# A two-layer hybrid decoder on one core: the adaLN vectors of the gates and of the shared K/V move from TensorE strips to VectorE sums, and one pair of gates moves to the last head

## The chip, the core and the metric

The kernel runs on one core of a Trainium2 chip. The metric is the device time of one launch in microseconds (us). Before the change the median of three runs is 934.68 us (934.39 to 935.48). Engines are named as in the profile: PE is TensorE, PEld its weight loads, DVE VectorE, ACT ScalarE, POOL GpSimd, SP the queue that issues the large loads.

## The reference, cut to what matters

Two decoder layers on 256 tokens of width 1024. Layer 0 mixes with an mLSTM block of four heads, layer 1 with causal attention over shared K and V; each then has a mixture of 16 experts. Everything is conditioned on one vector c: a product with a 1024 x 14336 matrix gives 14 vectors of 1024, the shift, scale and gate of every sub-layer and the shift and scale of K/V.

```python
cond = jax.nn.silu(c) @ w_ada + b_ada            # 14 vectors of 1024
mods = cond[:, :n_layer_mod].reshape(B, DEPTH, 2, 3, D)   # 0-11
kv_mod = cond[:, n_layer_mod:].reshape(B, 2, D)           # 12, 13
for layer in range(DEPTH):
    shift, scale, gate = mods[:, layer, 0, 0], mods[:, layer, 0, 1], 1.0 + mods[:, layer, 0, 2]
    h = x * (1 + scale) + shift
    y = mlstm_layer(h, ...) if layer == 0 else moba_layer(h, ..., shared K/V)
    x = layer_norm(DEEPNORM_ALPHA * x + gate * y, ...)
    shift, scale, gate = mods[:, layer, 1, 0], mods[:, layer, 1, 1], 1.0 + mods[:, layer, 1, 2]
    y = moe_ffn(x * (1 + scale) + shift, ...)
    x = layer_norm(DEEPNORM_ALPHA * x + gate * y, ...)
```

So vector 3i is a shift, 3i+1 a scale and 3i+2 a gate: 2 and 5 are the gates of layer 0, 8 and 11 those of layer 1, and 12, 13 are shift and scale of K/V.

## The kernel before, in words

The tokens lie in two tiles of 128. The program has four stretches: the start and the mLSTM of layer 0 (to about 316 us), its experts (to about 535 us), the attention of layer 1 (to about 691 us) and its experts. In the two mixers every weight tile (512 KB, loaded on SP's queue into a ring of 20 slots) is split in two halves: ScalarE copies the high part (L265), VectorE subtracts it for the low part (L266), and TensorE makes three matmuls of each product (L274, L275, L276).

Between these products the 14 conditioning vectors are worked off, each from 8 tiles of 128 x 1024 of w_ada. Vectors 0 and 1 come first. For the others there are two ways:

- `ada_vector` (L353): VectorE multiplies a tile by a column of silu(c) (L360) and adds seven more to it (L362); three steps later TensorE sums over the partitions with a block of ones, in four strips of 32 output partitions (L368); `ada_columns` (L340) copies that to an SBUF tile `mr` on ScalarE (L343), two steps later turns it by transposes (L348), and VectorE adds the bias (L350).
- `ada_pair` (L372): TensorE multiplies the tiles of two vectors as they come, four strips of 32 output partitions for each of 8 steps (L379, tile `adapp`), with nothing on VectorE. A pair of gates stays in rows in a tile `hl` (L387, L388); the pair (12, 13) goes through `ada_columns`.

A gate is spread to all partitions by `gate_rows` (L433): two matmuls for each half of 512 (L439), and one pass on ScalarE (L440).

The order of this work is set by `pump` (L402), which is called before every step of the large products: it gives a running vector a credit of RATE for each call, starts a pair when the count of calls reaches the pair's number, and moves what waits for its transposes one step on. `queue` (L426) sets what is to be done: 3, 4, 6, 7 by vectors and the pairs (2, 5) at call 8 and (12, 13) at call 46 in layer 0; 9, 10 by vectors and the pair (8, 11) at call 20 in layer 1. What is left over is worked off at once by `ada_all` (L418), which is called in `before_moe` (L456) and just behind it, ahead of the last products of a mixer (L935, L936 and L1519, L1520).

```python
RATE = (0.25, 0.33, 0.33)
PAIRS = ((2, 5, 8), (12, 13, 46)), ((8, 11, 20),)
```

Of the kernel before, what the change touches and what calls it, by code (L numbers as in the profile page):

```python
# [9 lines left out]
F32 = mybir.dt.float32  # L10
# [25 lines left out]
EXTRA = 4  # L36
RATE = (0.25, 0.33, 0.33)
PAIRS = ((2, 5, 8), (12, 13, 46)), ((8, 11, 20),)
WA = 3
# [118 lines left out]
def _body(ctx, tc, x, w_ada, a_w_in, a_wq, a_wk, a_wv, a_w_out, b_w_kv, b_wq, b_wo, moe_w_gate, moe_w_up,  # L158
# [161 lines left out]
    A.activation(csil, csil, AF.Silu)  # L320
    gaterow = {}
    before = keep.tile([P, P], BF16, name="before")
# [17 lines left out]
    def ada_columns(j, n, ps):  # L340

        mr = small.tile([P, P * n], F32, tag=("cv" if n == 2 else "lntmp"), name=f"mr{j}")
        A.copy(mr, ps)  # L343
        yield 0
        yield 0
        pt = bankB(f"adat{j}")
        for b in range(n):
            T.transpose(pt[:, P * b:P * b + P], mr[:, P * b:P * b + P], ident)  # L348
        o = slice(KD * j, KD * j + 4 * n)
        V.tensor_tensor(mod.rearrange("p j k -> p (j k)")[:, o].rearrange("p (g b) -> p g b", g=4),  # L350
                        pt[:, 0:P * n].rearrange("p (b g z) -> p g b z", b=n, g=4)[:, :, :, 0],
                        K("bada")[:, o].rearrange("p (g b) -> p g b", g=4), op=OP.add)

    def ada_vector(j, delay=3):
# [14 lines left out]
        busy.clear()  # L369
        yield from ada_columns(j, 2, ps[:, 0:256])  # L370

    def ada_pair(j, i):  # L372
# [12 lines left out]
        else:  # L385
            hl = keep.tile([P, 512], F32R, tag="shared", name=f"mr{j}")
            A.copy(hl, ps)  # L387
            V.scalar_tensor_tensor(hl, hl.bitcast(F32), C("low"), ps, op0=OP.mult, op1=OP.add)  # L388
            gaterow[j], gaterow[i] = (hl, 0), (hl, 2)

# [42 lines left out]
    def gate_rows(j):  # L433
        gt = keep.tile([P, D], F32, tag="gate", name=f"gate{j}")
        hl, g = gaterow[j]
        for h in range(2):
            pg = bankB(f"adag{j}_{h}")
            for r, v in ((16 + 2 * (j // 3) + h, lnr), (24 + g + h, hl)):
                T.matmul(pg, pick[:, r:r + 1].to_broadcast([P, P]), v, start=(v is lnr), stop=(v is hl))  # L439
            A.activation(gt[:, 512 * h:512 * h + 512], pg, AF.Identity, bias=ones)  # L440
# [370 lines left out]
    for _ in start_dense(3, range(1, 3)):  # L811
        pass
    queue((3, 4, 6, 7), RATE[0], PAIRS[0])
    for h in range(1, NH):
# [650 lines left out]
    with tc.issue_after(end.ins):  # L1465
        queue((9, 10), RATE[2], PAIRS[1])
        k_part(0)
# [100 lines left out]
```

## Time and profile before

| | |
|---|---|
| median of 3 runs | 934.68 us (934.39 to 935.48) |
| profiled execution: its time, its span | 936.49 us, 934.8 us |
| TensorE busy, mean granted clock | 884.2 us (95%), 0.980 |
| VectorE, ScalarE busy | 497.2 us (53%), 330.1 us (35%) |
| DMA | 318.57 MB, 341 GB/s over the span |

Matmuls are pipelined and the profile models their ends, so a share of 95% on TensorE says that something is in the array, not that it works at its peak. The shares are means over four stretches with different limits; so the stretches are read one by one, and within them the idle time of an engine together with what ended it.

### The profile page before, as it was taken

The numbers are of one execution on the slowest core, as the hardware profiler recorded it, in microseconds if no ns is written. First come the engines' busy times: TensorE is split into PE (matmuls) and PEld (weight loads), VectorE is DVE, ScalarE is ACT, GpSimd is POOL, SyncE is SP. The second block draws the span as 40 slices with busy tenths as digits, with TensorE's granted clock in tenths as the row PEclk, the third lists the DMA queues.
The fourth block names the chain that finished last, engine by engine and source line by source line (L and its number), as shares of the span: only waits on it lengthen the run. The fifth ranks groups of instructions, "written<-read, shape, count | busy, mean of one in ns | idle before, by whom it ended". The sixth has DMA issues, their size and how long they took to land. (4 is left out here: it accounts for less than half of the span.)

```text
span 934.8 us, 13546 instructions
## 1 busy us (share of the span) xinstructions
PE 884.2 (95%) x5141; PEld 537.4 (57%) x5144; DVE 497.2 (53%) x929; ACT 330.1 (35%) x547; POOL 7.8 (1%) x21
## 2 busy tenths in 40 slices
PE   9998999998999799999999889999979999999975
PEld 4885798695877544434343369577755443434322
DVE  2475877477788743233333289478675323333317
ACT  3465565364657311111111046376642111111110
POOL 0020000000000000000000000000000000000000
PEclk9999999998999999999999999999998999999988
DMA  9999976499757969999999999985685999999991
GB/s 329 390 392 406 351 266 218 135 393 392 254 196 272 359 237 407 407 405 407 407 407 406 377 410 416 412 301 207 250 313 210 407 406 407 406 407 407 407 393 59
DMA packets 161921, 318.57 MB, mean 341 GB/s; under 512 B 10120, under 2 KB 28168, under 8 KB 161848
## 3 DMA queue, kind: packets, MB, share of 16 engines
q1 hardware_dynamic: 161704, 317.42, 90.3%
q8 instruction: 43, 0.70, 0.3%
q14 instruction: 30, 0.25, 0.1%
q10 hardware_dynamic: 144, 0.20, 0.1%
HBM read 316.53 MB, written 1.05 MB: 340 GB/s over the span
## 5 line engine op out<-in xcount | busy, mean ns | idle before, releaser
L135 PE MATMUL py<-w,aT 128*64 128x512 f32 (+1 forms) x576 | 118.4, 554 | 1.7 <-DMA w<-in_moe_w_down_dram 1.7
L135 PE MATMUL pu<-w,xe 128*64 128x512 f32 x512 | 118.5, 596 | 0.1
L135 PE MATMUL pg<-w,xe 128*64 128x512 f32 x512 | 116.1, 596 | 0.0
L1221 DVE SCALAR_TENSOR_TENSOR yl<-py,wsl,yh 128x512 fp32r<-128x512 f32 x28 | 21.0, 750 | 177.7 <-ACT yh L1220 177.7
L135 PEld LDWEIGHTS py<-w,aT 128*64 128x64 f32 x576 | 41.3, 139 | 74.6 <-issue 62.5
L135 PEld LDWEIGHTS pu<-w,xe 128*64 128x64 f32 x512 | 36.0, 137 | 67.1 <-issue 61.3
L135 PEld LDWEIGHTS pg<-w,xe 128*64 128x64 f32 x512 | 34.8, 137 | 64.0 <-issue 58.9
L1187 ACT COPY aT<-aT 128x512 f32<-128x512 f32 x16 | 9.4, 586 | 143.6 <-PE aT L135 143.6
L530 DVE TENSOR_TENSOR lntmpe<-po,gate 128x512 f32<-128x512 f32 x56 | 36.1, 685 | 39.9 <-PE po L135 39.9
L362 DVE SCALAR_TENSOR_TENSOR adacc<-ada,pk,adacc 128x1024 f32<-128x1024 f32 x42 | 53.7, 1278 | 0.2
L1220 ACT ACTIVATE yh<-py,wsl 128x512 fp32r<-128x512 f32 x28 | 19.2, 687 | 85.1 <-PE py L135 85.1
L508 ACT ACTIVATE xe<-ga,coef 128x256 f32<-128x256 f32 x32 | 16.1, 561 | 73.2 <-PE ga L135 63.2
L274 PE MATMUL z<-hh,wz 128*128 128x256 f32 x128 | 37.0, 289 | 0.0
L275 PE MATMUL z<-hl,wz 128*128 128x256 f32 x128 | 36.1, 282 | 0.0
L531 DVE TENSOR_TENSOR xt<-xt,lntmpe 128x512 f32<-128x512 f32 x56 | 36.0, 683 | 0.0
L276 PE MATMUL z<-hh,wz 128*128 128x256 f32 x128 | 36.0, 281 | 0.0
L135 PE MATMUL ga<-onehot,xh 128*128 128x256 f32 x128 | 31.8, 327 | 0.0
L379 PE MATMUL adapp<-ada,pk 128*32 128x512 f32 x192 | 30.5, 599 | 0.0
L1180 DVE TENSOR_TENSOR a<-a,pu 128x512 f32<-128x512 f32 x16 | 11.0, 689 | 36.0 <-PE pu L135 35.6
L135 PE MATMUL xm<-hh,win 128*128 128x256 f32 x144 | 28.8, 289 | 0.7 <-ACT hh L135 0.7
L135 PEld LDWEIGHTS ga<-onehot,xh 128*128 128x128 f32 x128 | 25.3, 223 | 5.6 <-DVE xt L531 4.1
L274 PE MATMUL y<-wo,av 128*128 128x512 f32 x60 | 24.7, 415 | 3.4 <-ACT av L270 3.4
(386 smaller groups left out, 1899.9 us busy)
## 6 DMA issues: line engine op xcount, KB each, us to landing
w<-in_moe_w_gate_dram SPq DMA_DIRECT2D x128, 512.0 KB, 10.2
w<-in_moe_w_up_dram SPq DMA_DIRECT2D x128, 512.0 KB, 10.2
w<-in_moe_w_down_dram SPq DMA_DIRECT2D x128, 512.0 KB, 10.2
ada<-in_w_ada_dram SPq DMA_DIRECT2D x112, 512.0 KB, 9.7
win<-in_a_w_in_dram SPq DMA_DIRECT2D x16, 512.0 KB, 8.4
wz<-in_a_w_in_dram SPq DMA_DIRECT2D x16, 512.0 KB, 6.6
wout<-in_a_w_out_dram SPq DMA_DIRECT2D x16, 512.0 KB, 7.1
wv<-in_a_wv_dram SPq DMA_DIRECT2D x8, 512.0 KB, 5.7
```

Of the source, the lines that this page charges most:

```text
L135: return self.tc.keep_in_program_order(f(*a, **kw))
L274: T.matmul(ps, l[0], r[0], start=start, stop=False, skip_group_check=True)
L275: T.matmul(ps, l[0], r[1], start=False, stop=False, skip_group_check=True)
L276: T.matmul(ps, l[1], r[0], start=False, stop=stop, skip_group_check=True)
L362: V.scalar_tensor_tensor(acc, w, c, acc, op0=OP.mult, op1=OP.add)
L379: T.matmul(ps[32 * g:32 * g + 32, :], csil[:, k:k + 1].to_broadcast([P, 32]), w[g // 2][:, 512 * (g % 2):512 * (g % 2) + 512], start=(k == ...
L508: A.activation(dst, ps, AF.Identity, bias=sh[:, k:k + 1], scale=sc[:, k:k + 1])
L530: V.tensor_tensor(tmp, y, gate[:, c], op=OP.mult)
L531: V.tensor_tensor(dst[:, t, c], dst[:, t, c], tmp, op=OP.add)
L1180: V.tensor_tensor(a, a, pu, op=OP.mult)
L1220: A.activation(yh, py, AF.Copy, scale=wsl[:, b:b + 1])
L1221: V.scalar_tensor_tensor(yl, py, wsl[:, b:b + 1], yh.bitcast(F32), op0=OP.mult, op1=OP.subtract)
```

## The change

In layer 0 vectors 12 and 13 are now made as 3, 4, 6 and 7 are, by VectorE; the pair (2, 5) stays on TensorE but starts at call 44. In layer 1 no pair is left: 8, 9, 10 and 11 are all made by VectorE, the gates 8 and 11 side by side in one tile `hl`. RATE goes up. `mr` has its own buffer (in work[0], where it was one of `small`'s shared ones), and the transposes come six steps after the copy, not two. The number of tiles and bytes loaded in each layer stays.

```diff
-RATE = (0.25, 0.33, 0.33)
-PAIRS = ((2, 5, 8), (12, 13, 46)), ((8, 11, 20),)
+RATE = (0.45, 0.35, 0.55)
+PAIRS = ((2, 5, 44),), ()
...
-        mr = small.tile([P, P * n], F32, tag=("cv" if n == 2 else "lntmp"), name=f"mr{j}")
+        mr = work[0].tile([P, P * n], F32, tag="mr", name=f"mr{j}")
         A.copy(mr, ps)
-        yield 0
-        yield 0
+        for _ in range(6):
+            yield 0
...
-        yield from ada_columns(j, 2, ps[:, 0:256])
+        if is_gate(j):
+            if j % 2 == 0:
+                gates.append(keep.tile([P, 512], F32R, tag="shared", name=f"mr{j}"))
+            gate_parts(j, gates[-1][:, 256 * (j % 2):256 * (j % 2) + 256], ps[:, 0:256], range(4))
+        else:
+            yield from ada_columns(j, 2, ps[:, 0:256])
+
+    def is_gate(j):
+        return j < 12 and j % 3 == 2
+
+    def gate_parts(j, hl, ps, groups):
+
+        A.copy(hl, ps)
+        V.scalar_tensor_tensor(hl, hl.bitcast(F32), C("low"), ps, op0=OP.mult, op1=OP.add)
+        gaterow[j] = hl, groups
...
-            hl = keep.tile([P, 512], F32R, tag="shared", name=f"mr{j}")
-            A.copy(hl, ps)
-            V.scalar_tensor_tensor(hl, hl.bitcast(F32), C("low"), ps, op0=OP.mult, op1=OP.add)
-            gaterow[j], gaterow[i] = (hl, 0), (hl, 2)
+            gate_parts(j, keep.tile([P, 512], F32R, tag="shared", name=f"mr{j}"), ps, (0, 1))
+            gaterow[i] = gaterow[j][0], (2, 3)
...
     def gate_rows(j):
...
-            for r, v in ((16 + 2 * (j // 3) + h, lnr), (24 + g + h, hl)):
-                T.matmul(pg, pick[:, r:r + 1].to_broadcast([P, P]), v, start=(v is lnr), stop=(v is hl))
+            r = 16 + 2 * (j // 3) + h
+            T.matmul(pg, pick[:, r:r + 1].to_broadcast([P, P]), lnr, start=True, stop=False, skip_group_check=True)
+            for i in range(n):
+                r = 24 + groups[n * h + i]
+                T.matmul(pg[:, 512 // n * i:512 // n * i + 512 // n], pick[:, r:r + 1].to_broadcast([P, P]), hl, start=False, stop=(i == n - 1),
+                         skip_group_check=True)
...
-    queue((3, 4, 6, 7), RATE[0], PAIRS[0])
+    queue((3, 4, 12, 13, 6, 7), RATE[0], PAIRS[0])
...
-        queue((9, 10), RATE[2], PAIRS[1])
+        queue((8, 9, 10, 11), RATE[2], PAIRS[1])
```

The order of instructions shows where the pieces now stand. The first place is TensorE's queue in the q product of head 0. Before:

```order
L274 MATMUL q_1_866<-ch_731,wq_0_867 128x256
L379 MATMUL adapp_943<-ada_0_00_944,pk 32x512 x2
L379 MATMUL adapp_943<-ada_0_00_946,pk 32x512 x2
L275 MATMUL q_0_865<-cl_732,wq_0_867 128x256
L276 MATMUL q_0_865<-ch_731,wq_0_867 128x256
```

Changed:

```order
L274 MATMUL q_1_866<-ch_731,wq_0_870 128x256
L275 MATMUL q_0_865<-cl_732,wq_0_870 128x256
L276 MATMUL q_0_865<-ch_731,wq_0_870 128x256
L274 MATMUL q_0_865<-ch_731,wq_0_870 128x256
L275 MATMUL q_0_865<-cl_732,wq_0_870 128x256
```

The four strips of the pair (2, 5) are gone from here and from nine other places in the q and k products of heads 0 and 1; all of them now stand together before the last head's k product, where those of (12, 13) stood.

The second place is VectorE's queue in layer 1, behind the splits of the first q product (`adacc` is a vector's sum, `qs` and `sb` belong to the attention's scores). Before:

```order
L266 TENSOR_TENSOR bq_4_5473<-wq_1_00_5407,bq_4_5473 128x1024
L266 TENSOR_TENSOR bq_6_5533<-wq_1_01_5409,bq_6_5533 128x1024
L1418 TENSOR_SCALAR qs_5085<-bq_0_5411 128x512
L1418 TENSOR_SCALAR qs_5086<-bq_1_5412 128x512
L1430 SCALAR_TENSOR_TENSOR sb_5578<-group_384_5088,s_5579 128x384
```

Changed:

```order
L266 TENSOR_TENSOR bq_4_5487<-wq_1_00_5412,bq_4_5487 128x1024
L266 TENSOR_TENSOR bq_6_5517<-wq_1_01_5414,bq_6_5517 128x1024
L360 TENSOR_SCALAR adacc_5468<-ada_0_00_5469,pk 128x1024
L383 SCALAR_TENSOR_TENSOR mr_5465<-mr_5465,cs,adaps_5460 128x256
L362 SCALAR_TENSOR_TENSOR adacc_5468<-ada_1_00_5472,pk,adacc_5468 128x1024
L266 TENSOR_TENSOR bv_0_5603<-wv_0_00_5593,bv_0_5603 128x1024
L362 SCALAR_TENSOR_TENSOR adacc_5468<-ada_2_00_5502,pk,adacc_5468 128x1024
L362 SCALAR_TENSOR_TENSOR adacc_5468<-ada_3_00_5532,pk,adacc_5468 128x1024
L266 TENSOR_TENSOR bv_2_5621<-wv_0_01_5595,bv_2_5621 128x1024
L1435 TENSOR_SCALAR qs_5084<-bq_0_5416 128x512
```

Four pieces of vector 9, the second half of gate 8 and two splits of the next product now stand ahead of `qs`.

The third place is VectorE's queue at the end of layer 0's mixer, between the last splits of w_out and the first residual sum (`lntmpm`). Before:

```order
L266 TENSOR_TENSOR wo_21_3007<-wout_1_01_2986,wo_21_3007 128x1024
L909 TENSOR_TENSOR sz_2849<-sz_2849,u_2908 128x256
L466 TENSOR_TENSOR wrt_3023<-pk,coef 128x128 x2
L271 TENSOR_TENSOR axc_2883<-sz_2849,av_2882 128x512
L469 TENSOR_REDUCE rb<-rb_3026 128x32
```

Changed:

```order
L362 SCALAR_TENSOR_TENSOR adacc_2926<-ada_3_00_2981,pk,adacc_2926 128x1024
L271 TENSOR_TENSOR axc_2852<-sz_2818,av_2851 128x512
L362 SCALAR_TENSOR_TENSOR adacc_2926<-ada_4_00_2987,pk,adacc_2926 128x1024
L483 TENSOR_TENSOR wrt_3006<-pk,coef 128x128 x2
L362 SCALAR_TENSOR_TENSOR adacc_2926<-ada_5_00_3013,pk,adacc_2926 128x1024
L486 TENSOR_REDUCE rb<-rb_3009 128x32
L362 SCALAR_TENSOR_TENSOR adacc_2926<-ada_6_00_3016,pk,adacc_2926 128x1024
L488 SCALAR_TENSOR_TENSOR wr<-rb,wrt_3006 128x128
L362 SCALAR_TENSOR_TENSOR adacc_2926<-ada_7_00_3019,pk,adacc_2926 128x1024
L547 TENSOR_TENSOR lntmpm_3139<-y_0_2289,gate_2993 128x512
```

All eight pieces of vector 7, which were done before this place, now stand in it: the flush of `ada_all` works them off here. The eight pieces of vector 11 stand in the same place of layer 1.

## Rows read from the trace of the kernel before

**Rows 1.** The page's first part: busy time, share of the span, instructions.

```profile
PE 884.2 (95%) x5141; PEld 537.4 (57%) x5144; DVE 497.2 (53%) x929; ACT 330.1 (35%) x547; POOL 7.8 (1%) x21
```

**Rows 2.** Windows: stretch, length, busy of each engine, granted clock, DMA share, GB/s.

```profile
60.00:316.00 256.00, 244.38 (x1586) 193.22 (x1586) 186.90 (x297) 144.06 (x198) 0.64 (x4) 0.99 0.82 298
316.00:535.00 219.00, 211.24 (x1025) 89.11 (x1024) 75.63 (x174) 36.28 (x62) 0.00 (x0) 0.98 1.00 382
535.00:691.00 156.00, 149.80 (x973) 115.62 (x973) 119.25 (x213) 84.95 (x181) 0.00 (x0) 0.99 0.87 334
691.00:934.00 243.00, 222.81 (x1099) 96.71 (x1098) 91.98 (x212) 40.35 (x70) 0.00 (x0) 0.96 0.91 349
...
220.00:230.00 10.00, 5.92 (x20) 2.61 (x18) 8.81 (x16) 5.59 (x11) 0.00 (x0) 0.74 1.03 389
...
535.00:583.00 48.00, 43.82 (x332) 39.20 (x333) 44.22 (x75) 24.61 (x42) 0.00 (x0) 0.96 1.04 411
```

**Rows 3.** PE's waits, 60 to 330 us: waiter, releaser, us in total, times, longest.

```profile
PE pp L1054 <- DVE mask L1048: 3.5, 1, 3.5
PE y L274 <- ACT av L270: 3.4, 1, 3.4
PE adat L348 <- ACT mr L343: 2.4, 2, 1.8
```

**Rows 4.** Windows of tile adapp alone (the pairs): PE, PEld, DVE, ACT.

```profile
60.00:135.00 75.00, 11.42 (x64) 1.74 (x64) 0.75 (x1) 0.59 (x1) 1.00 0.96 363
165.00:190.00 25.00, 9.15 (x64) 2.20 (x64) 0.00 (x0) 0.59 (x1) 1.00 0.46 149
580.00:620.00 40.00, 9.97 (x64) 1.82 (x64) 0.75 (x1) 0.59 (x1) 1.00 1.01 396
```

**Rows 5.** PE's timeline around one half step of the pair (2, 5): start, us.

```profile
88.18 0.28 PE L275 MATMUL k<-cl,wk 128*128 128x256 f32 x1
88.39 1.05 PE L379 MATMUL adapp<-ada,pk 128*32 128x512 f32 x4
89.37 0.38 PE L276 MATMUL k<-ch,wk 128*128 128x256 f32 x1
```

**Rows 6.** Tiles adacc and mr: durations in ns (least, median, most).

```profile
L368 PE MATMUL adaps<-adacc,ones x48: 379/390/403, 140.9 to 662.8; 128*32 128x256 f32 x48
L362 DVE SCALAR_TENSOR_TENSOR adacc<-ada,pk,adacc x42: 1254/1279/1286, 71.0 to 647.4; 128x1024 f32<-128x1024 f32 x42
L360 DVE TENSOR_SCALAR adacc<-ada,pk x6: 745/748/753, 70.2 to 608.2; 128x1024 f32<-128x1024 f32 x6
...
L439 PE MATMUL adag<-mr,pick x8: 392/396/500, 300.1 to 695.3; 128*128 128x512 f32 x8
```

**Rows 7.** DVE's timeline: its two longest idle times in the mixers (in brackets).

```profile
92.75 1.23 DVE L271 TENSOR_TENSOR cl<-xc,ch 128x1024 fp32r<-128x1024 f32 x1 [11.14 <-ACT ch L270]
...
595.30 1.40 DVE L1418 TENSOR_SCALAR qs<-bq 128x512 f32<-128x512 f32 x2 [11.68 <-PE bq L276]
```

**Rows 8.** DVE's timeline at the end of layer 0's mixer.

```profile
294.20 1.23 DVE L266 TENSOR_TENSOR wo<-wout,wo 128x1024 fp32r<-128x1024 f32 x1 [0.40 <-ACT wo L265]
296.24 0.88 DVE L908 SCALAR_TENSOR_TENSOR u<-xc,group,u 128x256 f32<-128x256 f32 x2 [0.81 <-ACT u L907]
...
305.65 0.69 DVE L530 TENSOR_TENSOR lntmpm<-y,gate 128x512 f32<-128x512 f32 x1 [0.31 <-PE y L276]
...
317.00 0.81 DVE L549 TENSOR_SCALAR xt<-xt,lnmvm,lnrsm 128x1024 f32<-128x1024 f32 x1 [0.62 <-PE th L978]
```

**Rows 9.** DVE's timeline at the end of layer 1's mixer.

```profile
670.22 1.23 DVE L266 TENSOR_TENSOR bo<-wo,bo 128x1024 fp32r<-128x1024 f32 x1 [1.40 <-ACT bo L265]
674.41 0.42 DVE L1463 TENSOR_TENSOR ol__5276<-bo,oh__5275 128x256 fp32r<-128x256 f32 x1 [2.96 <-ACT oh__5275 L1462]
677.43 1.23 DVE L266 TENSOR_TENSOR vv_wo<-wo,vv_wo 128x1024 fp32r<-128x1024 f32 x1 [2.60 <-ACT vv_wo L265]
...
680.29 0.69 DVE L530 TENSOR_TENSOR lntmpm<-by,gate 128x512 f32<-128x512 f32 x1 [0.64 <-PE by L276]
```

**Rows 10.** Windows late in layer 1's mixer and behind it: PE, granted clock, DMA share.

```profile
640.00:660.00 20.00, 19.21 (x101) 1.00 0.31 117
...
691.00:710.00 19.00, 14.32 (x89) 0.82 0.40 152
```

More of the change, by code (lines that the diff above doesn't have):

```diff
@@ L320, in _body @@
     A.activation(csil, csil, AF.Silu)
-    gaterow = {}
+    gaterow, gates = {}, []
     before = keep.tile([P, P], BF16, name="before")
@@ L434, in gate_rows @@
         gt = keep.tile([P, D], F32, tag="gate", name=f"gate{j}")
-        hl, g = gaterow[j]
+        hl, groups = gaterow[j]
+        n = len(groups) // 2
         for h in range(2):
             pg = bankB(f"adag{j}_{h}")
-            for r, v in ((16 + 2 * (j // 3) + h, lnr), (24 + g + h, hl)):
-                T.matmul(pg, pick[:, r:r + 1].to_broadcast([P, P]), v, start=(v is lnr), stop=(v is hl))
+            r = 16 + 2 * (j // 3) + h
[4 more added lines that the diff above has]
+                         skip_group_check=True)
             A.activation(gt[:, 512 * h:512 * h + 512], pg, AF.Identity, bias=ones)
```

## The prediction

> **What bounds the kernel now.** The page's shares come first: PE is busy 95% of the span, VectorE 53% [rows 1]. A share over the span hides the stretches, so the windows by stretch are next [rows 2]. In layer 0's mixer (60 to 316 us) PE is busy 244.4 of 256 us and DMA at 0.82; in layer 1's (535 to 691 us) 149.8 of 156 and 0.87. In the experts' stretches DMA stands at 1.00 and 0.91. The reader is to see that the mixers have room on DMA and the experts hardly any. Third come PE's waits: in 60 to 330 us the three largest are 3.5, 3.4 and 2.4 us, and none of these is on a DMA [rows 3]. So the mixers go by PE's queue, and what leaves that queue shortens them, unless the engine that takes it over becomes late. That engine is VectorE: 186.9 of 256 us and 119.3 of 156 us busy there [rows 2], 73% and 76%. Last come VectorE's own idle times: 11.1 us at 92.75 and 11.7 us at 595.30 [rows 7]. Both end on a product whose steps are interleaved with a pair's strips (the first by way of ScalarE), so VectorE lies idle just where PE does the pairs.
>
> I sum against the profiled execution, 936.49 us; the median of the runs, 934.68, is 1.8 us lower, and the same difference is taken from the median. What a measurement of this kernel can tell from no change is about 0.2%, or 1.9 us.
>
> **What PE loses.** The pairs are busy 11.42, 9.15 and 9.97 us in their stretches [rows 4]. That busy time is halted products: between the two k matmuls around a half step lie 89.37 - 88.18 = 1.19 us where the strips show 1.05 [rows 5], and a step without strips is no longer than the 0.28 us of the row above. The pair (2, 5) leaves the q and k products: -11.4. It takes the place of (12, 13), with the same number of strips: 0 there, since the same 9.15 us stay. The pair (8, 11) goes: -10.0.
>
> **What PE gains.** Vectors 12, 13, 8 and 11 each add eight L368 records of 390 ns [rows 6]. Between four strips side by side (two rounds, 0.8 us) and one after the other (3.1 us) I take 0.8, since the pairs' 64 records of some 0.6 us take only 9 to 11 us together [rows 4]: 4 x 0.8 = +3.2. The transposes are as many as before, four for two vectors. Gates 8 and 11 take eight matmuls of 256 columns in place of four of 512 at 396 ns [rows 6]: from 0 more (half the time each) to 1.6 (the same time each); nearest are the L275 matmuls of 256 columns, 0.28 us [rows 5], so 8 x 0.28 - 4 x 0.40 = +0.6. PE's queue is then 11.4 + 10.0 - 3.2 - 0.6 = **17.6 us** shorter.
>
> Turning later: PE waits 2.4 us for `mr` at two transposes [rows 3]. Six steps instead of two let ScalarE's copy come first, and the own buffer takes away its wait for a user of `small`. What is late next is the product behind it, so I credit half: -1.2 (0 to -2.4).
>
> **What VectorE takes over.** A vector costs 0.748 + 7 x 1.279 = 9.7 us [rows 6], four cost 38.8, half in each layer. In layer 0's mixer VectorE is then busy 206.3 of about 246 us, 84%; in layer 1's 138.7 of about 147, 94%. Its idle 11.1 and 11.7 us [rows 7] are the cover: the order shows vector 9's first pieces and two splits moved ahead of `qs`, in the second of these. But this idle time exists because PE was slow there; without the pair it is shorter by the pair's time, and the rest has to come from many small pieces. The cost is PE waiting for a split (L266) or a low half (L271) behind a 1.28 us piece. Below it is 0. Above it is the whole of 17.6. Nearest is 535 to 583 us, where VectorE is already at 92% and PE is busy only 43.8 of 48 us [rows 2]: 4.2 us idle against the 2% that PE idles at best, so about 3 us per 48 at such a load. Layer 0 at 84% gets 1.5 us, layer 1 another 2: +3.5. Of the clock the rows say that in 220 to 230 us, where PE waited 3.4 us at once [rows 3], the granted clock was 0.74 of 2.4 GHz [rows 2], so part of it at 1.2; the waits I expect are single pieces of 1.3 us, and I add nothing for the clock.
>
> **The ends of the two mixers.** Vector 7 now falls into the flush, between the last w_out splits and the first residual sum. There VectorE is nearly full: from 294.20 to 305.65 us the larger idle pieces are 0.40, 0.81 and 0.31 [rows 8]. So its 9.7 us delay that place by up to 9.7 - 1.5 = 8.2 us; but PE still has its products of the last head to do while VectorE adds, the residual sums then run without waiting for PE, and VectorE's queue to the router (last row of rows 8) has waits that take up some of it. Ends 0 and 8.2; I take 2.5, because the queue ahead of the residual sums is PE's as well and the sums of the second token tile waited for PE before. In layer 1 vector 11 stands in the same place, but there VectorE idles 1.40 + 2.96 + 2.60 + 0.64 = 7.6 us [rows 9]: 9.7 - 7.6 = 2.1, ends 0 and 9.7; I take +2.1.
>
> **DMA.** The same tiles are loaded in each layer. In layer 1 vector 11's eight stand ahead of the experts' first weights on SP's queue and hold their ring slots until the flush. DMA is at 0.31 in 640 to 660 us and 0.40 in 691 to 710 us [rows 10], so the ring was full and waiting; the idle share there, (1 - 0.40) x 19 = 11 us, covers eight tiles that come in later (4.2 MB at 411 GB/s [rows 2] take 10 us). 0 (0 to +3).
>
> Sum: -17.6 - 1.2 + 3.5 + 2.5 + 2.1 = **-10.7 us**. Profiled: 925.8; median: **924.0 us**. Of it layer 0 gives -11.4 + 1.6 - 1.2 + 1.5 + 2.5 = -7.0 and layer 1 -10.0 + 1.6 + 0.6 + 2.0 + 2.1 = -3.7.
>
> The trace shows the strips overlapping: 64 records of about 0.6 us, 38 us in all, within 9 to 11.4 us [rows 4]. The Trainium skill, TensorE: Matmul & The Clock Gate, section "Part 3: Packing small matmuls — row/col tiling", says that matmuls on separate column groups run together, so that a pack takes one matmul's time plus about 4 ns for each further tile. It speaks against the change, as a packed pair would be cheaper on PE than it looks: by that rule 16 packs of 0.59 + 0.01 us make 9.6 us per pair, an estimate, and the change would remove 19.2 instead of 21.4 us. The trace's 9.15 and 9.97 agree with it, and 11.42 is above it.
>
> **Rivals.** *All cover holds.* The VectorE pieces fit into its idle time and the flushes delay nothing: -17.6 - 1.2 = -18.8, so 915.9. For it: 256 - 186.9 = 69 us of idle VectorE in layer 0 [rows 2]. Against it: 94% in layer 1, and 0.81 as the largest gap of rows 8.
>
> *VectorE becomes the bound.* If at 92% and more every split is late, layer 1 is worth only its VectorE time: the stretch has 138.7 us of it, and at the 92% that 535 to 583 us reached it needs 150.8 us, -5.2; with the flush on top (+9.7 - 7.6 = 2.1) and layer 0's flush at its upper end (8.2, so -1.3 for layer 0) it is -5.2 + 2.1 - 1.3 = -4.4: 930.3. For it: the row at 92%. Against it: in that row PE also waits for layer 1's start.
>
> *DMA is the bound.* If the weight stream sets the end of every stretch, the same bytes give the same time, 934.7. For it: 1.00 and 0.91 in the experts' stretches, 0.82 and 0.87 in the mixers [rows 2]. Against it: no large PE wait on a DMA in the mixer [rows 3], and 0.31 and 0.40 [rows 10]. The Trainium skill, Perfetto Trace Analysis, section "Identifying the Most-Contended Engine", says that TensorE's busy share is no good measure, and that DMA is to be judged by the use of HBM; by it PE's 95% proves nothing and the stream could be what counts. The trace agrees in part: DMA is at its full share in the experts.
>
> *The flushes decide, slower.* One mechanism: the chain from the last split to the router waits for whole vectors, 7 and 11, in VectorE's queue. If none of the eight pieces finds cover, each layer pays 9.7 us, 19.4 together; with the 3.5 of late splits the sum is -18.8 + 3.5 + 19.4 = +4.1, 938.8. It decides from the point where the two flushes cost over 15.3 us together. For it: the pieces stand ahead of the first `lntmpm` in order. Against it: the 7.6 us of idle in layer 1.
>
> **Chances.** Forecast (920 to 928) 0.52; all cover holds 0.12; VectorE the bound 0.18; DMA the bound 0.08; flushes decide 0.10. Slower by over 0.2% takes the last, same takes DMA's 0.08 and 0.02 of VectorE's tail: faster 0.80, same 0.10, slower 0.10. The range goes from 913 (all cover, with 2.4 for the waits and half of the 3.2 for L368) to 935 (DMA): what it leaves out is the flush case and some 0.08 at either end.
>
> **What would show it.** Right: L379's records fall from 192 to 64, all in one stretch near 170 us; both idle times of rows 7 are gone or under 3 us; VectorE's busy time is 497 + 39 = 536 us, PE's about 884.2 - 21.4 + 3.8 = 867; the router's `mask` comes about 7 us earlier in layer 0 and 11 us earlier in layer 1; the experts' stretches keep their lengths. Wrong: PE waits on L266 or L271 summing to over 8 us (VectorE the bound); lntmpm waiting for L362 by its full eight pieces in both layers (flushes); the experts' first matmul waiting for w (DMA).

## The result: 28.7 us faster, nearly three times the forecast

The changed kernel takes 905.86 us (median; three of four runs lie between 905.34 and 905.93, one at 911.9) against 934.53 us: a ratio of 0.9708, 95% interval 0.9666 to 0.9751. The forecast was 924.0, its range 913 to 935. The direction was right, the size was not.

The page of the changed kernel, first part, answers to [rows 1]: TensorE is busy 26 us less, VectorE 32 us more.

```profile
PE 858.2 (95%) x5049; PEld 533.3 (59%) x5052; DVE 529.1 (59%) x963; ACT 331.4 (37%) x550; POOL 7.8 (1%) x21
```

The windows by stretch, with columns as in [rows 2], at the same four boundaries of the work:

```profile
60.00:300.30 240.30, 231.66 (x1545) 191.98 (x1543) 201.66 (x305) 145.06 (x201) 0.64 (x4) 0.99 0.84 304
300.30:519.00 218.70, 210.58 (x1019) 88.33 (x1020) 77.21 (x184) 36.70 (x62) 0.00 (x0) 0.98 1.04 396
519.00:664.60 145.60, 139.12 (x930) 113.89 (x928) 134.75 (x228) 84.90 (x182) 0.00 (x0) 0.99 0.92 346
664.60:903.00 238.40, 222.04 (x1099) 96.64 (x1100) 92.32 (x213) 40.67 (x70) 0.00 (x0) 0.98 0.95 364
```

Layer 0's mixer went from 256.0 to 240.3 us, layer 1's from 156.0 to 145.6, the last stretch from 243.0 to 238.4; the first experts kept theirs. VectorE stands at 201.7 of 240.3 us and at 134.8 of 145.6: 84% and 93%, where 84% and 94% were forecast. A sharper mark is the mask that ends the router's chain. Its row in the kernel before, then in the changed one (first and last start in us):

```profile
L1048 DVE SCALAR_TENSOR_TENSOR mask<-gn,en x2: 191/192/192, 324.7 to 700.1; 128x32 bf16<-128x32 f32 x2
```

```profile
L1065 DVE SCALAR_TENSOR_TENSOR mask<-gn,en x2: 191/192/192, 309.0 to 673.8; 128x32 bf16<-128x32 f32 x2
```

Layer 0's mark comes 15.7 us earlier (forecast 7.0), the time from mark to mark falls from 375.4 to 364.8 (10.6; forecast 3.7), and from the second mark to the end of the span it falls from 234.7 to 230.3 (4.4; forecast 0). Together 30.7 of span, for 28.7 between the medians, most of the rest because the profiled execution of before was 1.8 us above its median.

What TensorE waits for in 60 to 330 us now, the three largest, answering to [rows 3]. The wait of the transposes for `mr` and that of y are gone; the one for the mask is 1.6 us longer, the one for `hn` (the heads' normalisation) was 0.5 us before, and none is on the split of a weight.

```profile
PE pp L1071 <- DVE mask L1065: 5.1, 1, 5.1
PE hnT L919 <- ACT hn L899: 3.9, 2, 3.5
PE q L275 <- DVE cl L271: 1.8, 1, 1.8
```

The instructions of the vectors, answering to [rows 6]: 70 + 10 of VectorE's in place of 42 + 6, of unchanged length.

```profile
L362 DVE SCALAR_TENSOR_TENSOR adacc<-ada,pk,adacc x70: 1250/1279/1286, 71.4 to 653.6; 128x1024 f32<-128x1024 f32 x70
L360 DVE TENSOR_SCALAR adacc<-ada,pk x10: 744/748/754, 70.6 to 638.6; 128x1024 f32<-128x1024 f32 x10
```

The gain can be split by what TensorE did. Two windows of each execution, from 60 us to the first mark and from mark to mark, before and then changed:

```profile
60.00:324.70 264.70, 248.61 (x1619) 195.63 (x1619) 192.31 (x328) 150.43 (x210) 0.64 (x4) 0.99 0.83 302
324.70:700.10 375.40, 361.48 (x1999) 205.09 (x2000) 195.04 (x386) 121.47 (x243) 0.00 (x0) 0.99 0.94 360
```

```profile
60.00:309.00 249.00, 235.49 (x1574) 193.90 (x1573) 208.56 (x344) 151.84 (x213) 0.64 (x4) 0.99 0.85 307
309.00:673.80 364.80, 350.58 (x1955) 203.34 (x1957) 211.03 (x404) 121.74 (x244) 0.00 (x0) 0.99 0.99 376
```

TensorE's busy time falls by 13.1 and 10.9 us. The pairs' strips are most of that: 8.32 us are left in layer 0 of 11.42 + 9.15 [rows 4], and none of the 9.97 in layer 1. TensorE's idle time (the length less the busy time) goes from 16.1 to 13.5 us and from 13.9 to 14.2, although VectorE has four more vectors to add.

The forecast had not looked at the order of SP's queue either. From 48 us the kernel before issued this (start, length of the issuing, tile, count; 512 KB each; two rows of two tiles are left out):

```profile
48.72 17.40 SPq L224 DMA_DIRECT2D ada<-in_w_ada_dram  x15
67.02 2.58 SPq L224 DMA_DIRECT2D wv<-in_a_wv_dram  x2
...
74.46 10.57 SPq L224 DMA_DIRECT2D ada<-in_w_ada_dram  x7
85.13 3.59 SPq L224 DMA_DIRECT2D win<-in_a_w_in_dram  x4
```

and the changed kernel this:

```profile
48.75 3.12 SPq L224 DMA_DIRECT2D ada<-in_w_ada_dram  x5
52.86 2.05 SPq L224 DMA_DIRECT2D wv<-in_a_wv_dram  x2
...
60.91 6.64 SPq L224 DMA_DIRECT2D ada<-in_w_ada_dram  x5
69.55 3.48 SPq L224 DMA_DIRECT2D win<-in_a_w_in_dram  x4
```

Between the first head's weights and the tiles of `win` stood 15 + 7 tiles of w_ada, and now 5 + 5. Twelve tiles are 6.3 MB, 15.3 us at the 410 GB/s at which the stream ran there; `win` is issued 15.6 us earlier. The window of the kernel before that shows this is finer than the ones the forecast used:

```profile
60.00:100.00 40.00, 36.90 (x241) 27.28 (x241) 28.70 (x44) 25.92 (x38) 0.22 (x2) 1.00 1.03 410
100.00:160.00 60.00, 59.49 (x427) 49.42 (x426) 44.69 (x57) 32.99 (x44) 0.41 (x2) 1.00 0.78 271
160.00:200.00 40.00, 38.38 (x293) 30.42 (x292) 22.49 (x31) 19.90 (x25) 0.00 (x0) 1.00 0.62 216
```

The mean of 0.82 over layer 0's mixer is 1.03 in 60 to 100 us, 0.78 and 0.62 behind it. The stream was full first and had room later.

But a full stream is not yet a wait. Head 1's `wv` in the kernel before: the issues, the time from issue to landing, and the start of the first split:

```profile
L224 SPq DMA_DIRECT2D wv<-in_a_wv_dram x2: 378/378/378, 67.0 to 69.2; - x2
DMA to landing us min/median/max: 9.9/9.9/9.9
93.10 1.05 ACT L265 CAST wv<-wv 128x1024 fp32r<-128x1024 f32 x1
```

The weights had landed by about 79 us, 14 us before ScalarE split them. From 60 to 130 us the profile of this kernel puts no wait of TensorE, VectorE or ScalarE down to a load.

### The profile page after: what moved, and what is told of

The parts are those of the page before. It is cut to its first block, busy times and chain, and to the rows that moved or that the text cites. A ratio compares the mean times of both kernels' runs of the same rounds, so it can differ in the third digit from the quotient of the medians.

```text
span 904.1 us, 13441 instructions
## 1 busy us (share of the span) xinstructions
PE 858.2 (95%) x5049; PEld 533.3 (59%) x5052; DVE 529.1 (59%) x963; ACT 331.4 (37%) x550; POOL 7.8 (1%) x21
## 3 DMA queue, kind: packets, MB, share of 16 engines
HBM read 316.53 MB, written 1.05 MB: 351 GB/s over the span
## 4 chain that ended last, share of the span: by engine, by line
PE 40%; DMA 10%; DVE 3%; ACT 2%; issue 1%; DVEq 0%; SPq 0%; ACTq 0%
PE py L135 8%; PE pg L135 8%; PE pu L135 7%; DMA w<-in_moe_w_up_dram 3%; DMA w<-in_moe_w_down_dram 3%; PE ga L135 3%; PE po L135 2%; DMA ada<-in_w_ada_dram 2%; DMA w<-in_moe_w_gate_dram 1%; PE bo L1477 1%; PE bk L275 1%; PE by L274 1%; PE bk L276 1%; PE bk L274 1%; PE by L276 1%
## 5 line engine op out<-in xcount | busy, mean ns | idle before, releaser
L362 DVE SCALAR_TENSOR_TENSOR adacc<-ada,pk,adacc 128x1024 f32<-128x1024 f32 x70 | 89.4, 1278 | 0.4
L525 ACT ACTIVATE xe<-ga,coef 128x256 f32<-128x256 f32 x32 | 16.1, 562 | 73.0 <-PE ga L135 63.0
L1192 ACT ACTIVATE a<-pg 128x512 f32<-128x512 f32 x16 | 9.6, 597 | 52.2 <-PE pg L135 52.2
L135 PE MATMUL ga<-onehot,xl 128*128 128x256 f32 x128 | 27.7, 283 | 0.0
## 6 DMA issues: line engine op xcount, KB each, us to landing
wout<-in_a_w_out_dram SPq DMA_DIRECT2D x16, 512.0 KB, 10.1
```

The lines of the kernel that those rows point to most:

```text
L135: return self.tc.keep_in_program_order(f(*a, **kw))
L362: V.scalar_tensor_tensor(acc, w, c, acc, op0=OP.mult, op1=OP.add)
L525: A.activation(dst, ps, AF.Identity, bias=sh[:, k:k + 1], scale=sc[:, k:k + 1])
L1192: A.activation(a, pg, AF.Silu)
```

## The experiments

All times are medians, the ratios with the kernel before on the same chip (934.5 to 935.3); "mark" is the start of `mask` in layer 0. A mark comes from one profiled execution: kernels with the same code up to it agree within 0.5 us where the granted clock went the same way, and differ by up to 3.3 where it did not.

### The parts one by one

Layer 0's part alone (the changed kernel with layer 1's lines of before):

```diff
-RATE = (0.45, 0.35, 0.55)
-PAIRS = ((2, 5, 44),), ()
+RATE = (0.45, 0.35, 0.33)
+PAIRS = ((2, 5, 44),), ((8, 11, 20),)
...
-        queue((8, 9, 10, 11), RATE[2], PAIRS[1])
+        queue((9, 10), RATE[2], PAIRS[1])
```

> Layer 0's part alone (12, 13 by VectorE, pair (2, 5) at call 44, the new turning); layer 1 with its pair (8, 11) on TensorE as before. Theory A (TensorE's queue is the whole price, VectorE's added work is covered): layer 0's mixer ends 15 to 16 us earlier, as in the changed kernel, layer 1's mixer keeps its length within 1 us, so 918 to 920 us if the branch near the end keeps its 5.9 us on TensorE, and 914 to 916 if not. Theory B (the mixers gain only what the strips were busy, 11 us, and the rest comes from the branch near the end): 923 with the long branch, 919 without it.

Measured 917.18 us, ratio 0.9824 (0.9787 to 0.9861); mark of layer 0 at 310.2, mark to mark 374.7, and a short branch at the end. Layer 0's mixer holds its 14.5 us alone.

Layer 1's part alone:

```diff
-RATE = (0.45, 0.35, 0.55)
-PAIRS = ((2, 5, 44),), ()
+RATE = (0.25, 0.33, 0.55)
+PAIRS = ((2, 5, 8), (12, 13, 46)), ()
...
-    queue((3, 4, 12, 13, 6, 7), RATE[0], PAIRS[0])
+    queue((3, 4, 6, 7), RATE[0], PAIRS[0])
```

> Layer 1's part alone (8, 9, 10, 11 by VectorE, no pair), layer 0's vectors and pairs as before but with the new turning. Theory A: layer 1's mixer is 10 to 11 us shorter, layer 0's 1 to 3 us, so 921 to 924 us with the long branch and 917 to 920 without it. A rival, that VectorE at 94% in layer 1 is paid for by an earlier start of the stream from layer 0's gain: layer 1's mixer gains only 4 to 6 us, 927 to 930.

Measured 919.84 us, ratio 0.9851 (0.9812 to 0.9890); mark to mark 364.9, that is 10.5 us, what the whole change gives there. TensorE's busy time from mark to mark is 351.4 us in place of 361.5, so 10.1 of the 10.5 are work that has left its queue. Layer 0's mark at 323.2 shows the new turning alone.

The turning alone, in the kernel before:

```diff
-        mr = small.tile([P, P * n], F32, tag=("cv" if n == 2 else "lntmp"), name=f"mr{j}")
+        pool = work[0] if n == 2 else small
+        mr = pool.tile([P, P * n], F32, tag=("mr" if n == 2 else "lntmp"), name=f"mr{j}")
         A.copy(mr, ps)
-        yield 0
-        yield 0
+        for _ in range(6 if n == 2 else 2):
+            yield 0
```

> The kernel before with only the turning changed: own buffer for the rows of one vector, six steps instead of two; the pair (12, 13) turns as before. Theory A: the two waits for mr (2.4 us) go in part, 0.5 to 2.5 us earlier, 932 to 934 us. Rival (the turning carries layer 0's gain above the strips, by freeing the buffer that VectorE's convolution uses): 4 us or more, 930 or less.

Measured 931.56 us, ratio 0.9971 (0.9948 to 0.9994); mark at 322.7, 2.0 us earlier (1.5 in the run above, which has the same code up to there). The two large parts add up to within a few us of the whole, so each can be studied by itself.

### What the strips cost

Seven of eight steps of the pair (2, 5) narrowed, in the kernel before:

```diff
+                n = 32 if (j == 2 and k) else 512
-                T.matmul(ps[32 * g:32 * g + 32, :], csil[:, k:k + 1].to_broadcast([P, 32]), w[g // 2][:, 512 * (g % 2):512 * (g % 2) + 512],
-                         start=(k == 0), stop=(k == KD - 1))
+                T.matmul(ps[32 * g:32 * g + 32, 0:n], csil[:, k:k + 1].to_broadcast([P, 32]), w[g // 2][:, 512 * (g % 2):512 * (g % 2) + n],
+                         start=(k == 0), stop=(k == KD - 1), skip_group_check=True)
```

> The kernel before with seven of the eight steps of the pair (2, 5) done on 32 columns a strip in place of 512 (leaves out most of the gates' product; loads, order and waits stay). If a strip costs the products what it was busy, 7/8 of 11.4 us less a rest of some 0.1 us a step: 9 us faster, mask of layer 0 at 315 to 316 us. If the halt costs more than that (12.9 us by the landmarks): 10 to 11 us faster, mask at 314. If VectorE's ease is what counts, layer 0 gains under 5.

Measured 932.53 us, ratio 0.9976 (0.9953 to 0.9999); mark at 322.1. The strips were busy 3.94 us in place of 11.42, and the mark came only 2.6 us earlier. The first v matmul of head 1, on TensorE's timeline of the kernel before and of this one:

```profile
95.03 0.71 PE L274 MATMUL v<-wv,mh 128*128 128x512 f32 x2
```

```profile
93.97 1.22 PE L274 MATMUL v<-wv,mh 128*128 128x512 f32 x2 [3.29 <-ACT wv L265]
```

It starts 1.1 us earlier, behind a wait of 3.3 us on the high half of its weights (L265). The expectation says that order and waits stay; they did not. ScalarE's timeline around that split, of the kernel before and of this one:

```profile
93.10 1.05 ACT L265 CAST wv<-wv 128x1024 fp32r<-128x1024 f32 x1
95.31 0.49 ACT L751 ACTIVATE sT<-sps 128x384 f32<-128x384 f32 x1 [1.17 <-PE sps L750]
95.70 0.59 ACT L722 ACTIVATE cv<-xm,group 128x256 f32<-128x256 f32 x1
```

```profile
90.53 0.49 ACT L752 ACTIVATE sT<-sps 128x384 f32<-128x384 f32 x1 [2.49 <-PE sps L751]
90.92 2.06 ACT L723 ACTIVATE cv<-xm,group 128x256 f32<-128x256 f32 x4
92.89 1.98 ACT L265 CAST wv<-wv 128x1024 fp32r<-128x1024 f32 x2
```

The split, ahead of `sT` and `cv` before, now stands behind them. Its weights were issued at 66.5 and 69.2 us and landed 9.3 us later, so TensorE waited for ScalarE's order and not for the stream. Around that wait the granted clock was 0.57 in 92 to 100 us, so mostly at 1.2 GHz, where it was 1.00 before. TensorE's idle time up to the mark is 18.8 us in place of 16.1. So the 2.6 us are what a saving of 7.5 us of busy time left after 2.7 us more idle time and up to 3.4 us of lower clock. They are no price of the strips alone, and all three readings of the expectation miss that.

The same in layer 1, with `j == 8` in place of `j == 2`:

> The kernel before with seven of the eight steps of the pair (8, 11) in layer 1 on 32 columns a strip (leaves out most of these gates' product; loads, order and waits stay). Theory P holds in layer 1 (strips are the price there): layer 1's mixer from mask to mask 375.4 us before, now 366 to 368, as its whole part of the change (364.9) almost. Theory L also here (the 16 loads are what counts): 372 or more.

Measured 933.32 us, ratio 0.9987 (0.9959 to 1.0015); mark to mark 375.2 against 375.4. The pair (8, 11) was busy 3.50 in place of 9.97 us and, within the interval (up to 4 us faster), nothing came of it. New waits of TensorE in 535 to 680 us, each on a split of the next weights:

```profile
PE bv L275 <- DVE bv L266: 1.5, 1, 1.5
PE bv L274 <- ACT bv L265: 0.8, 1, 0.8
```

ScalarE's timeline shows the same as in layer 0. The split of the first `wv` tile, at 584.15 us in the kernel before, here stands behind the scores of the attention, and ScalarE first waits 11 us for these:

```profile
596.02 0.40 ACT L1439 ACTIVATE sb<-sb,mx 128x128 f32<-128x128 f32 x1 [11.02 <-DVE mx L1437]
596.42 1.03 ACT L265 CAST bv<-wv 128x1024 fp32r<-128x1024 f32 x1
```

The four `wv` tiles were issued from 573.4 to 579.1 us and landed 8 to 10 us later, before this split. From mark to mark TensorE is idle 16.9 us in place of 13.9, and the granted clock was 0.57 in 549 to 557 us and in 600 to 604, where it was 0.79 and 1.00: up to 3.4 us more. Together that is about the 6.5 us of work that was taken away.

SP's queue differs too, between this kernel and layer 1's part alone, which gains 10.5 us. With the pair, 14 tiles of w_ada come in a row ahead of `wv`, without it 5, and `wv` is issued at 563.0 us in place of 573.4 (8.9 us sooner counted from each kernel's mark). As these weights lay ready before their split in both, this does not show the loads to be the cause. Moving them alone was not tried in layer 1.

### Where the pair stands

One number of the kernel before changed; nothing goes to VectorE:

```diff
-PAIRS = ((2, 5, 8), (12, 13, 46)), ((8, 11, 20),)
+PAIRS = ((2, 5, 40), (12, 13, 46)), ((8, 11, 20),)
```

> The kernel before with one number changed: the pair (2, 5) starts at call 40 in place of 8, so its 16 tiles and all its strips move behind head 2's weights; nothing goes to VectorE. Theory P (TensorE's queue is the price, as predicted): the same strips in another place, mask of layer 0 within 2 us of before (324.7), 933 to 936 us. Theory L (the place of the 16 loads is what counts: in 48 to 95 us the stream of weights is the bound): head 1's v product starts at about 85 us and not 95, mask 5 to 10 us earlier though every strip stays, 925 to 930 us.

Measured 930.27 us, ratio 0.9950 (0.9931 to 0.9969); mark at 317.6, 7.1 us earlier with all strips still there, as its theory L has it. Head 1's first v matmul:

```profile
86.04 0.40 PE L274 MATMUL v<-wv,mh 128*128 128x512 f32 x1
```

Nine us sooner, without a wait. But the strips moved with the loads, and up to that product they were busy 7.2 us in the kernel before. So this start does not tell the two theories apart. The same with the strips narrowed:

> The same with seven of the eight steps of the pair (2, 5) on 32 columns a strip (leaves out most of the gates' product). Against the same thinning with the loads left early, which gained 2.6 us in layer 0. Theory P: again 2 to 5 us, mask at 320 to 322. Theory L: now the strips' time is worth its full 8 to 10 us on top of the loads' move, mask at 309 to 312, 912 to 918 us.

Measured 919.79 us, ratio 0.9845 (0.9806 to 0.9884); mark at 307.5. The four kernels side by side, from 60 us to layer 0's mark. The last column is an estimate from the windows, their length times (1 - granted clock), and an upper bound, as a slow clock costs nothing while TensorE is idle:

| pair (2, 5) | mark, us | both pairs' strips busy | TensorE idle | lost at the lower clock |
|---|---|---|---|---|
| early (call 8), whole | 324.7 | 20.6 | 16.1 | 3.4 |
| early, narrowed | 322.1 | 13.3 | 18.8 | 6.9 |
| late (call 40), whole | 317.6 | 19.3 | 14.5 | 1.7 |
| late, narrowed | 307.5 | 13.6 | 12.5 | 0.0 |

Narrowing takes 5.7 to 7.3 us off TensorE's queue in either place. It moves the mark by 2.6 us where idle time and clock got worse and by 10.1 where both got better. The place is worth 7.1 us with whole strips: 1.3 of strips, 1.6 of idle time, up to 1.7 of clock, and some 2.5 in the other products, which stays open. With narrowed strips it is worth 14.6, and nearly all of that is idle time and clock. What the loads have to do with it is not shown: no run moves them and keeps the order of the other queues.

The other way round, the changed kernel with its pair early again:

```diff
-PAIRS = ((2, 5, 44),), ()
+PAIRS = ((2, 5, 8),), ()
```

> The changed kernel with the pair (2, 5) at call 8 again. Theory P: the strips cost 11.4 in place of 9.2 us, 907 to 909 us. Theory L: 17 tiles of w_ada stand ahead of head 1's weights again, head 1's v starts at about 95 us, layer 0's mixer gives back 8 us or more, 913 to 920 us.

Measured 921.42 us, ratio to before 0.9856 (0.9816 to 0.9895): 15.6 us given back by that number alone. Mark at 323.9, 14.9 us later: the strips are busy 13.3 us in place of 8.3, TensorE is idle 17.7 us in place of 13.5, and the granted clock (0.79 in 70 to 86 and in 102 to 110 us, 1.00 in both before) costs up to 5.0 us more. Theory L has the size right. Head 1's first v matmul waits again for a split that stands behind `cv` on ScalarE:

```profile
104.02 1.22 PE L274 MATMUL v<-wv,mh 128*128 128x512 f32 x2 [3.48 <-ACT wv L265]
```

### What VectorE's new work costs

The adding steps of vectors 8, 11, 12 and 13 narrowed in the changed kernel:

```diff
-                V.scalar_tensor_tensor(acc, w, c, acc, op0=OP.mult, op1=OP.add)
+                n = 32 if j in (12, 13, 8, 11) else D
+                V.scalar_tensor_tensor(acc[:, 0:n], w[:, 0:n], c, acc[:, 0:n], op0=OP.mult, op1=OP.add)
```

> The changed kernel with the seven adding steps of vectors 8, 11, 12 and 13 done on 32 of 1024 columns (leaves out most of these four sums; loads, order and waits stay). It takes some 34 us of VectorE's work away. Theory A (VectorE's added work is covered): within 2 us of the changed kernel, 904 to 906. Rival, the step of the prediction (late splits and flushes cost 8 us): 898 to 900.

Measured 902.36 us, 3.5 us below the changed kernel, which the two ratios' intervals do not separate; marks at 305.9 (3.1 earlier) and 363.7 from mark to mark (1.1 less). Some 34 us of VectorE's work cost about 4 us at the marks: between the two expectations. Vector 7, which the forecast's +2.5 is about, kept its full width here. Its flush shows in the last product of layer 0's mixer, in the kernel before, the changed one, and the one with RATE (0.45, 0.45, 0.55) of the last experiments, where vector 7 is done earlier:

```profile
312.44 0.40 PE L276 MATMUL y<-wo,axc 128*128 128x512 f32 x1
```

```profile
292.97 0.40 PE L276 MATMUL y<-wo,axc 128*128 128x512 f32 x1
```

```profile
300.84 0.39 PE L276 MATMUL y<-wo,axc 128*128 128x512 f32 x1
```

From its end to the mark (324.7, 309.0, 313.0) are 11.8, 15.6 and 11.8 us, so the flush delays the mark by 3.8 us. In layer 1 the same stretch is 11.8 and 11.9 us: nothing.

VectorE's limit shows in the changed kernel without any pair:

```diff
-RATE = (0.45, 0.35, 0.55)
-PAIRS = ((2, 5, 44),), ()
+RATE = (0.6, 0.45, 0.55)
+PAIRS = (), ()
...
-    queue((3, 4, 12, 13, 6, 7), RATE[0], PAIRS[0])
+    queue((3, 2, 4, 5, 12, 13, 6, 7), RATE[0], PAIRS[0])
```

> The changed kernel without any pair: gates 2 and 5 also by VectorE, RATE[0] 0.6 and RATE[1] 0.45, so that eight vectors fit. Theory A (TensorE's queue is the whole price): the cluster of 9.15 us near 160 us goes, two sums of 0.6 us come, 7 to 8 us faster than the changed kernel, about 898 us. Rival (VectorE becomes the bound): layer 0's mixer then asks VectorE for about 226 of its 232 us, splits come late, and the time is 906 or more.

Measured 919.85 us, 14 us above the changed kernel: the rival held. (About 2.5 of them lie behind the second mark, with a branch of 5.89 us, see below.) At 168 us it is ahead (head 3's score matmuls start there, with the changed kernel at 171); mark at 321.6, 12.6 us behind the changed kernel's. TensorE's timeline between shows two waits that the changed kernel has not at this size, one in the heads' normalisation, one at the end for a vector's sum:

```profile
225.91 0.69 PE L919 MATMUL hnT<-cs,hn 128*128 128x128 f32 x2 [6.35 <-ACT hn L899]
...
307.19 0.64 PE L368 MATMUL adaps<-adacc,ones 128*32 128x256 f32 x8 [3.15 <-DVE adacc L362]
```

TensorE is idle 25.9 us up to the mark in place of 13.5, and the clock costs up to 11.9 us in place of 1.7 (0.66 in 220 to 230 us, behind the first of these waits). How much of the 12.6 us is VectorE and how much is the clock is not separated.

### The branch near the end

Both kernels have a conditional block for experts with too many tokens, not entered here. Its branch in layer 1 on TensorE's queue (the PEld rows of that line from 840 us on), before and changed:

```profile
L1322 PEldq COMPARE_BRANCH  x1: 5890/5890/5890, 892.8 to 892.8; - x1
```

```profile
L1339 PEldq COMPARE_BRANCH  x1: 318/318/318, 866.6 to 866.6; - x1
```

and the matmul behind it, on TensorE's waits from 710 us on:

```profile
PE aT L135 <- PEq L1322: 4.7, 1, 4.7
```

```profile
PE aT L135 <- DVEq L1339: 1.0, 1, 1.0
```

It took 5.89 us and takes 0.32 (the 0.36 of the expectations below is the branch of layer 0). Without the block in layer 1 (`if AT[layer] >= b and layer == 0:` ahead of `rest()`), first the kernel before, then the changed one:

> The kernel before without the conditional block near its end (leaves out the overflow path of layer 1's experts, which this input does not take). Theory A (the branch's 5.9 us on TensorE, with 4.7 us of idle array and a lower clock behind it, is the last experts' difference): 4 to 7 us faster than before, 928 to 930 us, and its spread of 930 to 937 us shrinks to about 1 us. Rival (the stretch goes by the weight stream and the branch is hidden): within 1 us of before.

> The changed kernel without the same block (leaves out layer 1's overflow path). Theory A: its branch took 0.36 us, so within 1 us of the changed kernel, 904.5 to 906; against the kernel before without the block the change is then worth the mixers' 15.7 + 10.7 = 26 us less what the clock there gives, 24 to 26 us. Rival (the whole 29 us belong to the mixers and start of the stream): the pair differs by 28 us or more.

Measured 931.73 us, ratio 0.9959 (0.9941 to 0.9978), and 905.53 us, 0.3 below the changed kernel. Without the block the two kernels are 26.2 us apart, so some 2.5 to 3.5 us of the 28.7 hang on this branch and the rest does not. The spread of the kernel before did not shrink (929.0 to 934.1): that part of the expectation was wrong.

Tiny matmuls at the start, to move the changed kernel's code (92, then 46 of them):

```diff
     stay_warm(FILL[0], 0)
+    pw = bankB("padw")
+    for _ in range(92):
+        tc.keep_in_program_order(T.matmul(pw[:, 0:8], onesq.to_broadcast([P, P]), onesq.to_broadcast([P, 8]), start=True, stop=True))
```

> The changed kernel with 92 tiny matmuls (8 columns) after the first warm-up, so that TensorE's program has as many instructions ahead of the last branch as in the kernel before. If the branch's length hangs on where its code lies: 5.9 us at the branch and some 4 to 6 us slower than the pads alone make it (the pads show in the mask of layer 0, 309.0 before). If not: 0.36 us at the branch.

> The same with 46 tiny matmuls: as many instructions as in the runs of layer 0's or layer 1's part alone, whose branch took 0.36 and 0.46 us. By place of code: short, under 0.5 us. If it is chance: either.

Measured 908.95 and 907.95 us with branches of 1.58 and 0.33 us; the first is neither of the two values that its expectation names. The kernel with only the turning changed had 1.59 us, those with one part alone 0.32 and 0.33, and the changed kernel without pairs 5.89. What makes it long stays open.

### Other rates

Four more settings of RATE, (0.35, 0.45, 0.55), (0.45, 0.45, 0.55), (0.35, 0.35, 0.55) and (0.45, 0.35, 0.45), in this order:

> The changed kernel with RATE (0.35, 0.45, 0.55) in place of (0.45, 0.35, 0.55): fewer of w_ada's tiles ahead of the early weights, more of them between z and w_out. Theory L: the early products start 1 to 2 us sooner, and the flush of vector 7 stays; 903 to 906 us. Rival (VectorE is what counts behind 200 us, as all_vectors showed): slower than the changed kernel by 2 us or more.

> The changed kernel with RATE[1] 0.45 in place of 0.35: the early loads stay as they are, more of vectors 6 and 7 is done before the flush at layer 0's end. If the 3 us lost with (0.35, 0.45, 0.55) came from this stretch: 907 to 909. If they came from the early stretch and the flush of vector 7 costs 1 to 2 us: 903.5 to 905.

> The changed kernel with RATE[0] 0.35 in place of 0.45: 3 of w_ada's tiles fewer ahead of the early weights, 11 in place of 6 behind the last w_out weights, so more for the flush. Theory L, early loads decide: early products 1 to 2 us sooner and 903 to 905. Rival, the flush decides there: vector 6's rest and all of vector 7 (up to 13 us of VectorE) stand on the chain to the router, mask of layer 0 later than 311, 908 or more.

> The changed kernel with RATE[2] 0.45 in place of 0.55: in layer 1 four of w_ada's tiles fewer between the weights, 12 in place of 8 behind w_o. Theory L: layer 1's mixer, 364.8 us from mask to mask with the changed kernel, goes to 361 to 363. Rival, the flush decides: 366 to 369, 907 to 910.

Measured 908.74, 908.20, 909.25 and 909.79 us: 2.3 to 3.9 us above the changed kernel, less than the intervals of their ratios (about 4 us either way) can tell. Part of that is no matter of RATE: the last has layer 0's code unchanged, and its mark was at 312.3 in place of 309.0. The windows of 70 to 86 us show a cause, first of the changed kernel, then of this one:

```profile
70.00:86.00 16.00, 13.30 (x102) 12.25 (x101) 15.96 (x23) 13.69 (x21) 0.11 (x1) 1.00 0.93 353
```

```profile
70.00:86.00 16.00, 13.28 (x84) 12.60 (x83) 15.46 (x22) 11.13 (x18) 0.11 (x1) 0.79 0.94 362
```

The granted clock was 0.79 there, so part of it at 1.2 GHz, behind the 1.8 us wait for `cl` that both have. In layer 1 the clock cost both about the same (0.99 and 0.98 from mark to mark), and there the flush shows. With 12 tiles of w_ada behind `wo` in place of 8, mark to mark is 366.5 us for RATE[2] 0.45 against 364.8, and from the last product to the mark 15.9 us against 11.9. So the flush that its rival names is there, at 1.7 us, but the median holds the clock's loss in layer 0 too. In layer 0 the clock covers what RATE did. (0.45, 0.45) took the flush away, 3.8 us, and its mark was at 313.0 with a granted clock of 0.96 from 60 us to the mark, against 0.99. The 11 tiles of (0.35, 0.35) put the mark to 314.1, at 0.98. None of these runs beats the changed kernel, and none shows that these RATEs could not.

## Why the prediction was wrong, step by step

The forecast was -17.6 us for TensorE's queue and +6.9 for its waits (-1.2 + 3.5 + 2.5 + 2.1), and nothing behind the second mark. Measured, between the two profiled executions:

| | forecast, us | measured, us |
|---|---|---|
| TensorE busy, both mixers and the stretch between the marks | -17.6 | -24.0 |
| TensorE idle, the same | +6.9 | -2.3 |
| behind the second mark | 0 | -4.4 |
| sum | -10.7 | -30.7 |

**The waits, "+3.5", "+2.5", "+2.1" and "-1.2": the step that failed.** The sum put the cost of VectorE's new work on top of the waits that were there, and let only half of one of these go. TensorE's idle time did not grow by 6.9 us, it fell by 2.3: from 16.1 to 13.5 in layer 0, and from 13.9 to 14.2 in layer 1. In layer 1 the terms of 2.0 and 2.1 were mis-sized: narrowing both new vectors gives 1.1 us there, and the flush shows nothing. In layer 0 VectorE costs more than forecast, 3.1 us for vectors 12 and 13 and 3.8 for the flush, against 1.5 and 2.5. What outweighs it is that waits of the kernel before went with the change: y for `av` (3.4 us, with the clock at 0.74 around it), `mr` (2.4), `pgcol` (1.6 to 0.2). Which part of the change took which of them is shown for `mr` and y alone, which the new turning shortens (y to 0.8, with `hn` at 3.7 in its stead). The rest stays open. The idle 11.7 us before `qs` went away as forecast, filled by vector 9's pieces.

**The strips, "-11.4" and "-10.0": right as work.** 20.57 us of strips became 8.32 and 9.97 became none, so 12.3 and 10.0 us left TensorE's queue. The sums of the vectors cost 1.9 us more on it in place of 3.2. Some 4 us of the 24.0 are in the other products, at most 1.7 of them by the clock. By the Trainium skill, TensorE: Matmul & The Clock Gate, "Part 3: Packing small matmuls — row/col tiling", the prediction had 9.6 us per pair as an estimate. The measured pairs go from 8.3 us, standing together, to 13.3, among the products of the changed kernel with its pair early.

**The place of the pair: not priced.** The text has the pair (2, 5) "take the place of (12, 13)" at its busy time. Moving it back costs 14.9 us at the mark in the changed kernel, of which the strips are 5.0, idle time 4.2 and the granted clock up to 5.0. In the kernel before, moving it out gives 7.1.

**DMA, "0 (0 to +3)"**: not refuted. The change takes 12 tiles out of the full stretch of SP's queue, and the share of 1.03 there was not in the text. But the weights lay ready 14 us before their split, and no run separates their place from that of the strips.

**Turning, "-1.2 (0 to -2.4)"**: 1.5 to 2.0 at the mark. Right within its ends.

**Behind the second mark**: 4.4 us where the lengths were to stay, 2.5 to 3.5 of it with the branch, which is not in the sum.

**The clock, nothing added.** It is not the main term between these two executions, but it is in every comparison of the runs. That the change came out with less of it than most of its variants is luck as far as the runs show.

**The rivals.** "DMA is the bound" is wrong: the same bytes took 28.7 us less. The Trainium skill, Perfetto Trace Analysis, section "Identifying the Most-Contended Engine", says that TensorE's busy share is not a good measure of how close a kernel is to its limit, from which the prediction took that the stream could be what counts. The trace does not bear that out in 60 to 130 us, where no wait of a compute engine is put down to a load. "All cover holds" came nearest (915.9), and the waits did not grow; 6.4 us more off TensorE's queue and the last stretch made the rest. "The flushes decide" is real at 3.8 us in layer 0 and nothing in layer 1. "VectorE becomes the bound" showed only with eight vectors in layer 0.

## What to carry to other kernels

Split a measured gain into busy time, idle time and granted clock of the engine that is changed before naming a cause; here the strips were forecast well and the waits were not. To call a stream of loads the bound, show a consumer that waits for a tile which has not landed; a share of 1.03 does not show it. To price some work by narrowing it, compare the order of the other queues and the clock as well: here both narrowed kernels had a split in another place, so the small gain is not the price of the strips. Before giving work to an engine at 90%, count what is left over for the flush at the end of the stretch.

## What was not expected of the hardware

The branch around a block that is not entered took 0.32 to 5.89 us on TensorE's queue by the profile, with 4.7 us of idle array at the longest, in a stretch with DMA at 1.05. And behind the same wait of 1.8 us near 72 us the granted clock was 1.00, 0.89 or 0.79 in 70 to 86 us, in kernels with the same code there: with 0.79 the mark came 3.3 us later, with 0.89 about 1.0. What decides which of them it is, the runs do not show.
